# Attention: three kinds of store on another queue, a gating row loaded and used in one unit, more filler steps at the start, the last squares on another engine

## The chip, the cores and the metric

The kernel runs on one core of one Trainium2 chip. The core has five engines with instruction queues of their own: TensorE (PE: matmuls and transposes, with its weight loads shown as PEld), VectorE (DVE), ScalarE (ACT), GpSimd (POOL) and SyncE (SP, which only issues DMAs here). The metric is the device time of one execution in microseconds (us).

## The reference, cut to what matters

One layer: a norm, a combined input projection, three causal attention branches a, b and c, a gate and an up-projection for each, a merge by sigmoid gates gm, an output projection with a residual add and a last norm. SEQ and D_MODEL are 1024.

```python
h = rms_norm(x, norm_gain[l], RMS_EPS)
proj = jnp.einsum('bsd,de->bse', h, w_in[l])          # q, k, v, gates of a, b, c, and gm
ya = diff_attention(...)                              # 4 heads, two softmaxes each, width 128
ya = (rms_norm(ya, subln_gain[l], SUBLN_EPS) * (1.0 - lam_init)).reshape(B, S, A_WIDTH)
yb = sliding_window_attention(...)                    # 8 heads, window 128
yc = forgetting_attention(...)                        # 8 heads, decay by cumulated log gates
ua = jnp.einsum('bse,ed->bsd', ya * jax.nn.silu(ga), w_up_a[l])
ub = jnp.einsum('bse,ed->bsd', yb * jax.nn.silu(gb), w_up_b[l])
uc = jnp.einsum('bse,ed->bsd', yc * jax.nn.silu(gc), w_up_c[l])
gates = jax.nn.sigmoid(gm.reshape(B, S, N_BRANCH, D))
merged = gates[:, :, 0] * ua + gates[:, :, 1] * ub + gates[:, :, 2] * uc
x = x + jnp.einsum('bsd,de->bse', merged, w_o[l])
```

## The kernel before

Matmul operands are split into a high and a low part, so that most products are three matmuls (high by high, low by high, high by low). The program has three stretches: norm and projections, to about 518 us of the profile; attention, to 962 us, with 28 filler steps ahead of it from 518 us on; and up-projections, merge, output projection and last norm. The change lies in the attention stage.

**Units.** Attention runs over a list of units: 16 of part b (two groups of heads by eight row blocks), 32 of part c (eight heads by four pairs of row blocks) and 16 of part a (four heads h by pairs g = 3, 2, 1, 0). A unit is a list of score steps (L630 or L755 on PE, the maximum and mask on DVE in L650 or L757, the exponential on ACT), a list of transposes (L676, with the cast pt on ACT and the rest pt on DVE, L683) and a list of products with v (L709). The loop over units runs the scores of unit n beside the transposes and products of unit n - LAG, LAG being 2, so that the first two units have scores alone and the last two passes have none. Inputs q, k and v of a head are loaded some units ahead by SP (L608, L620) into buffers that are given free by PE.

**Fillers.** 16 tiles of the gm gates are left over from the projection stage and computed in between: `fillers()` is a generator of 256 steps of three matmuls each (L531 to L533). FILL_0 = 28 steps stand ahead of the first unit; then each step of a unit earns a fraction of a filler step (FILL_B, FILL_C, FILL_A by part), until FILL_END = 8 are left, which are kept for the last two passes. A finished half row is copied by ACT to gr (L537) and stored to gmd by DMA (L538).

**Gates of branch b.** When the last half rows have been computed (`cur["free"]`), the eight gating rows of branch b are worked off, GPART = 2 entries of the list gq at the head of each unit. `gate_load` (L560) loads a row of y (yd_b) into a buffer of tag y_st, and a row of silu values (sgd) into a buffer of tag w_st, in which filler weights are loaded too. `gate` multiplies them on DVE (L567), ACT casts the product (L101) and DVE takes the rest (L104). The list puts the load of row n + 1 ahead of the gate of row n.

**End of a unit of part a.** `store` in `part_a`: ACT copies the result to ya (L857), a DMA stores it to yd_a (L859), POOL squares it (L861), ACT casts the squares, POOL takes the rest (L104), and NSUM cost units later PE sums them by two matmuls (L867); ACT copies the sums (L868), and a DMA stores them to ssd (L869). gr, ya, y2, y_lo and the gating row share the five buffers of tag y_st.

**Order.** PE's instructions run in the order in which the program issues them. On the other engines the order is a scheduler's, so that an edit of one line can move others. All DMAs named here are issued by SP. Eight semaphores are shared by the DMAs in turn, and an issue waits until the DMA that had its semaphore before has landed.

Of the kernel before, what the change touches and what calls it, by code (L numbers as in the profile page):

```python
# [12 lines left out]
ALU = mybir.AluOpType  # L13
# [3 lines left out]
P = 128  # L17
# [18 lines left out]
LAG, AHEAD, TVLAG = 2, 3, 1  # L36
# [2 lines left out]
NLAST, GPART, NY, NSUM = 6, 2, 5, 8.0  # L39
GATE_AT = {"b": (0, 1, 2, 3, 4, 4, 5, 5), "c": (1, 1, 2, 2, 3, 4, 5, 5)}  # L40
FILL_END, FILL_Z = 8, 1.5
FILL_0, FILL_B, FILL_C, FILL_A = 28, 0.8, 0.6, 0.75
NPW, UPAHEAD, WARM = 3, 3, 14
UPS = [(br, d) for br in "bca" for d in range(NK)]
WO_AT = {5 + 2 * n: (m, t) for n, (m, t) in enumerate((m, t) for m in ((0, 0), 3, 2, (1, 0)) for t in range(2))}
# [4 lines left out]
def hybrid_block_kernel(ctx, tc, x, norm_gain, w_in, b_forget, lambda_q1, lambda_k1, lambda_q2, lambda_k2,  # L50
                        subln_gain, sinks, w_up_a, w_up_b, w_up_c, w_o, final_gain, out):
    nc = tc.nc
# [45 lines left out]
    def split(src, hi, lo, act=False, eng=nc.gpsimd):  # L98

        if act:  # L100
            first = nc.scalar.copy(hi, src)  # L101
        else:
            first = nc.gpsimd.tensor_scalar(out=hi, in0=src, scalar1=1.0, scalar2=1.0, op0=ALU.mult, op1=ALU.mult)
        return first, eng.tensor_tensor(lo, src, hi.bitcast(F32), ALU.subtract)  # L104
# [414 lines left out]
    def fillers():  # L519


        for tiles, halves in ([([t], (1, 0)) for t in DIRECT[:-NLAST]] + [(DIRECT[-NLAST:], (1,)), (DIRECT[-NLAST:], (0,))]):
            for bi, d in tiles:
                w = [operand(load_half(GM + bi * D + d * P, i)) for i in range(2)]
                for c in halves:
                    ps = cur["psum"]()
                    for i in range(2):
                        for k in range(4):
                            f, l = i == 0 and k == 0, i == 1 and k == 3
                            r = hb[i, c]  # L530
                            nc.tensor.matmul(ps, w[i][0][:, k, :], r[0][:, k, :], start=f, stop=False)  # L531
                            nc.tensor.matmul(ps, w[i][0][:, k, :], r[1][:, k, :], start=False, stop=False)
                            nc.tensor.matmul(ps, w[i][1][:, k, :], r[0][:, k, :], start=False, stop=l)  # L533
                            if l:
                                pool, tg, nb = cur["row"]
                                gr = pool.tile([P, 512], F32, name="gr", tag=tg, bufs=nb)
                                nc.scalar.copy(gr, ps)  # L537
                                nc.sync.dma_start(gmd[bi, d, :, c * 512:c * 512 + 512], gr)  # L538
                            yield
            if halves == (1,):  # L540
                cur["free"] = True
# [36 lines left out]
    with tc.tile_pool(name="at", bufs=2, reuse_waits="tile") as at, \  # L578
# [14 lines left out]
        def fill(n):  # L593
            owed[0] += n
            while owed[0] >= 1:
                owed[0] -= 1
                if left[0] > cur["keep"]:
                    left[0] -= 1
                    next(filler)
# [228 lines left out]
        def part_a(u, h, g):  # L828
# [25 lines left out]
            def store(y):  # L854

                ya = at.tile([P, 512], F32, name="ya", tag="y_st", bufs=NY)
                nc.scalar.copy(ya[:, :256], y[:, :256])  # L857
                cols = slice(g * 256, g * 256 + 256)
                nc.sync.dma_start(yd["a"][h * P:h * P + P, cols], ya[:, :256])  # L859
                y2 = at.tile([P, 2, 256], F32R, name="y2", tag="y_st", bufs=NY)  # L860
                nc.gpsimd.tensor_tensor(ya[:, 256:], ya[:, :256], ya[:, :256], ALU.mult)  # L861
                split(ya[:, 256:], y2[:, 0, :], y2[:, 1, :], True)

                def sums():
                    pn = cur["psum"]()
                    for t in range(2):
                        nc.tensor.matmul(pn[:2, :256], ones, y2[:, t, :], start=t == 0, stop=t == 1)  # L867
                    nc.scalar.copy(ya[:1, :256], pn[:1, :256])  # L868
                    nc.sync.dma_start(ssd[h:h + 1, cols], ya[:1, :256])  # L869
                after(NSUM, sums)  # L870
            ta, va = pv_pair(g, w, lhs, 3, store)
            return sa, ta, va, lambda: None
# [56 lines left out]
        def tick(c):  # L929
            clock[0] += c  # L930
            for e in list(later):
                if e[0] <= clock[0]:
                    later.remove(e)
                    e[1]()
        gq = [gb[0][0]] + [f for n in range(8) for f in ([gb[n + 1][0]] if n < 7 else []) + [gb[n][1]]]
        for n in range(len(units) + LAG):
            if "free" in cur:
                if "b" not in yg:
                    gate_tiles("b")
                for f in gq[:GPART]:  # L940
                    f()
                del gq[:GPART]

            while ahead < min(n + AHEAD + 1, len(units)):
                if units[ahead][0]:
# [23 lines left out]
            while sa or tv:  # L969
                if sa and (not tv or (ps_ + 0.5 * sa[0][0]) * ct <= (pt_ + 0.5 * tv[0][0]) * cs):  # L970
                    c, f = sa.pop(0)
                    ps_ += c
                else:
                    c, f = tv.pop(0)
                    pt_ += c
                f()
                if n < len(units):
                    fill(c * rate[kind] / 0.65)
                else:
                    cur["keep"] = 0  # L980
                    fill(c * FILL_Z / 0.65)
                tick(c * (1 + rate[kind]))
        for _, f in later:
            f()

# [170 lines left out]
```

## Time and profile before

| what | before |
|---|---|
| median of 3 timed runs | 1188.73 us (1188.29 to 1191.81) |
| profiled execution, its own time | 1184.62 us |
| its span, first to last instruction | 1182.8 us |
| mean granted clock of TensorE | 0.991 |
| PE busy | 1147.9 us, 97% |
| DVE busy | 815.4 us, 69% |
| POOL busy | 693.8 us, 59% |
| ACT busy | 585.5 us, 50% |

All times in the rows are microseconds from the start of the span, durations included, unless marked ns. Busy time of an engine is time in instructions that compute. A bracket at the end of a row, as [1.18 <-DMA qk<-qd], is the time for which the engine stood idle before it, and what ended the wait. Names read out<-in by the program's tiles. A granted clock of 1.00 is 2.4 GHz, one of about 0.5 is 1.2 GHz. SPq and ACTq are the queues from which SP and ACT issue DMAs.

### The profile page before, as it was taken

To read this page: it belongs to the slowest core of one execution; us is meant where nothing else is said; L and a number is where in the kernel's file an instruction comes from. 1 tells how busy PE (TensorE), PEld (TensorE's weight loads), DVE (VectorE), ACT (ScalarE), POOL (GpSimd) and SP (SyncE) were. 2 spreads that over 40 slices of the span, in tenths; PEclk is the share of its full clock that TensorE was granted. 3 is DMA by queue.
4 is the path that set the end of the run, shared out by engine and by line. 5 is a ranking of instruction groups with operands and counts; after the bars stand their busy time and mean duration, and the time that the engine had idled before them with its cause. 6 is when DMAs were issued, how large, how long until landed. Compare 5 with 4: busy or idle time off the path is not lost. (4 is left out here: it accounts for less than half of the span.)

```text
span 1182.8 us, 18767 instructions
## 1 busy us (share of the span) xinstructions
PE 1147.9 (97%) x5787; PEld 972.6 (82%) x5787; DVE 815.4 (69%) x1655; ACT 585.5 (50%) x1255; POOL 693.8 (59%) x684
## 2 busy tenths in 40 slices
PE   7999999999999999998999999999998999999997
PEld 6999888888888888887888888888877878888775
DVE  7767767768687775322887767768677835664898
ACT  6432333433444444323886666667877842334423
POOL 5056656657667676454556665766767732477643
PEclk8999999999999999999999999999999999999999
DMA  7442266666856555349946466466668359798322
GB/s 242 155 153 91 103 209 230 233 213 198 266 185 205 166 164 161 99 117 247 258 117 194 133 191 183 134 176 172 176 205 234 121 163 337 271 345 306 129 107 107
DMA packets 184531, 221.70 MB, mean 187 GB/s; under 512 B 16280, under 2 KB 116712, under 8 KB 182640
## 3 DMA queue, kind: packets, MB, share of 16 engines
q1 hardware_dynamic: 184288, 219.99, 58.9%
q8 instruction: 46, 0.75, 0.3%
q14 instruction: 53, 0.43, 0.1%
q10 hardware_dynamic: 144, 0.52, 0.1%
HBM read 144.89 MB, written 75.56 MB: 186 GB/s over the span
## 5 line engine op out<-in xcount | busy, mean ns | idle before, releaser
L104 POOL TENSOR_TENSOR w_lo<-w_st,w_hi 128x512 fp32r<-128x512 f32 x130 | 173.4, 1340 | 108.5 <-ACT w_hi L101 89.4
L104 POOL TENSOR_TENSOR w_lo<-w_sf,w_hi 128x512 fp32r<-128x512 f32 x96 | 143.2, 1494 | 104.8 <-ACT w_hi L101 84.4
L109 PE MATMUL pm<-t,w_hi 128*128 128x512 f32 x320 | 126.3, 395 | 0.7 <-ACT w_hi L101 0.7
L111 PE MATMUL pm<-t,w_lo 128*128 128x512 f32 x320 | 126.3, 395 | 0.0
L110 PE MATMUL pm<-t,w_hi 128*128 128x512 f32 x320 | 126.0, 394 | 0.0
L630 PE MATMUL sc<-qk 128*128 128x512 f32 (+2 forms) x384 | 101.9, 356 | 3.7 <-DVE m L650 3.7
L683 DVE TENSOR_TENSOR pt<-tp,pt 128x512 fp32r<-128x512 f32 x102 | 70.1, 687 | 23.8 <-ACT pt L682 23.0
L169 DVE TENSOR_TENSOR w_sf<-w_st 128x512 f32<-128x512 f32 x40 | 47.7, 1193 | 43.5 <-DMA w_st<-in_w_in_dram 34.8
L630 PEld LDWEIGHTS sc<-qk 128*128 128x128 f32 x384 | 64.6, 189 | 15.3 <-DVE m L650 6.8
L101 ACT CAST w_hi<-w_sf 128x512 fp32r<-128x512 f32 x96 | 58.5, 613 | 35.4 <-PE pm L110 29.5
L109 PEld LDWEIGHTS pm<-t,w_hi 128*128 128x128 f32 x320 | 60.1, 188 | 14.9 <-ACT w_hi L101 1.1
L110 PEld LDWEIGHTS pm<-t,w_hi 128*128 128x128 f32 x320 | 60.1, 188 | 14.1
L111 PEld LDWEIGHTS pm<-t,w_lo 128*128 128x128 f32 x320 | 60.1, 188 | 14.1
L101 ACT CAST w_hi<-w_st 128x512 fp32r<-128x512 f32 x86 | 51.3, 615 | 37.6 <-PE pm L110 28.5
L682 ACT CAST pt<-tp 128x512 fp32r<-128x512 f32 x102 | 59.4, 582 | 20.4 <-PE tp L676 18.8
L423 ACT ACTIVATE qk_hi<-u 128x512 fp32r<-128x512 f32 x32 | 20.2, 633 | 94.2 <-DVE u L191 43.9
L664 POOL TENSOR_SCALAR e_c<-e_c,r 128x1024 f32<-128x1024 f32 (+3 forms) x64 | 47.9, 749 | 23.8 <-DVE r L658 20.0
L709 PE MATMUL y<-pt,v 128*128 128x256 f32 x336 | 55.4, 290 | 2.4 <-DVE pt L683 2.2
L656 ACT ACTIVATE e_c<-e_c,m 128x1024 f32<-128x1024 f32 (+3 forms) x64 | 49.9, 780 | 13.7 <-DVE m L650 12.8
L840 POOL TENSOR_TENSOR e_a<-e_a,e_a 128x896 f32<-128x896 f32 (+7 forms) x32 | 47.3, 1481 | 15.9 <-ACT e_a L839 15.8
L656 ACT ACTIVATE e_a<-e_a,m 128x896 f32<-128x896 f32 (+7 forms) x64 | 49.6, 775 | 13.3 <-DVE m L650 13.1
L1048 POOL TENSOR_TENSOR mt<-mt,row 128x512 f32<-128x512 f32 x28 | 39.5, 1426 | 24.7 <-DVE row L1047 24.6
(299 smaller groups left out, 3511.4 us busy)
## 6 DMA issues: line engine op xcount, KB each, us to landing
w_st<-in_w_in_dram SPq DMA_DIRECT2D x126, 256.0 KB, 3.4
qk<-qd SPq DMA_DIRECT2D x224, 128.0 KB, 3.1
wo<-wod SPq DMA_DIRECT2D x14, 1024.0 KB, 9.0
row<-gmd SPq DMA_DIRECT2D x48, 256.0 KB, 4.5
qd<-qk_hi SPq DMA_DIRECT2D x42, 256.0 KB, 4.1
qd<-qk_lo SPq DMA_DIRECT2D x42, 256.0 KB, 4.9
vd<-vt SPq DMA_DIRECT2D x24, 384.0 KB, 2.3
v<-vd SPq DMA_DIRECT2D x9, 1024.0 KB, 9.8
```

Source lines behind the costliest of these rows:

```text
L101: first = nc.scalar.copy(hi, src)
L104: return first, eng.tensor_tensor(lo, src, hi.bitcast(F32), ALU.subtract)
L109: nc.tensor.matmul(ps, w[0][:, k, :], r[0][:, k, :], start=start and k == 0, stop=False)
L110: nc.tensor.matmul(ps, w[0][:, k, :], r[1][:, k, :], start=False, stop=False)
L111: nc.tensor.matmul(ps, w[1][:, k, :], r[0][:, k, :], start=False, stop=stop and k == n - 1)
L169: nc.vector.tensor_tensor(t, x, y, op)
L630: nc.tensor.matmul(ps[:, :n], q, kk[t][c][:, o:o + n], start=t == 0, stop=t == 1)
L656: nc.scalar.activation(e[:, :L], e[:, :L], AF.Exp, bias=m2, scale=-1.0, accum_out=den)
L664: nc.gpsimd.tensor_scalar(out=e, in0=e, scalar1=r, scalar2=1.0, op0=ALU.mult, op1=ALU.mult)
L682: nc.scalar.copy(pt[:, 0, a:], tp[:, a:])
L683: nc.vector.tensor_tensor(pt[:, 1, a:], tp[:, a:], pt[:, 0, a:].bitcast(F32), ALU.subtract)
L709: nc.tensor.matmul(y[:, :256], l_, r_, start=t == 0 and n == 0, stop=last and n == len(mms) - 1)
```

## The change

Three kinds of DMA are issued by ACT instead of SP: gr to gmd (32 of them), ya to yd_a (16) and the sums to ssd (16). In the list of gates the load of a row stands at the head of a unit and its gate at the end of the same unit, one row per unit. In the first two units a fixed number of two filler steps stands behind each of the eight score steps, and FILL_B and FILL_A are a little lower. In the last two units of part a (h = 3, g < 2) the squares and their rest are done by DVE instead of POOL.

```diff
-FILL_0, FILL_B, FILL_C, FILL_A = 28, 0.8, 0.6, 0.75
+FILL_0, FILL_S, FILL_B, FILL_C, FILL_A = 28, 2, 0.75, 0.6, 0.74
...
                                 nc.scalar.copy(gr, ps)
-                                nc.sync.dma_start(gmd[bi, d, :, c * 512:c * 512 + 512], gr)
+                                nc.scalar.dma_start(gmd[bi, d, :, c * 512:c * 512 + 512], gr)
...
-                nc.sync.dma_start(yd["a"][h * P:h * P + P, cols], ya[:, :256])
+                nc.scalar.dma_start(yd["a"][h * P:h * P + P, cols], ya[:, :256])
                 y2 = at.tile([P, 2, 256], F32R, name="y2", tag="y_st", bufs=NY)
-                nc.gpsimd.tensor_tensor(ya[:, 256:], ya[:, :256], ya[:, :256], ALU.mult)
-                split(ya[:, 256:], y2[:, 0, :], y2[:, 1, :], True)
+                eng = nc.vector if h == 3 and g < 2 else nc.gpsimd
+                eng.tensor_tensor(ya[:, 256:], ya[:, :256], ya[:, :256], ALU.mult)
+                split(ya[:, 256:], y2[:, 0, :], y2[:, 1, :], True, eng)
...
                     nc.scalar.copy(ya[:1, :256], pn[:1, :256])
-                    nc.sync.dma_start(ssd[h:h + 1, cols], ya[:1, :256])
+                    nc.scalar.dma_start(ssd[h:h + 1, cols], ya[:1, :256])
...
-        gq = [gb[0][0]] + [f for n in range(8) for f in ([gb[n + 1][0]] if n < 7 else []) + [gb[n][1]]]
+        gq = [f for n in range(8) for f in gb[n]]
         for n in range(len(units) + LAG):
+            gnow = []
             if "free" in cur:
                 if "b" not in yg:
                     gate_tiles("b")
-                for f in gq[:GPART]:
+                gnow = gq[:2]
+                del gq[:2]
+                for f in gnow[:1]:
                     f()
-                del gq[:GPART]
...
                 f()
-                if n < len(units):
+                if n < LAG:
+                    fill(FILL_S)
+                elif n < len(units):
                     fill(c * rate[kind] / 0.65)
...
+            for f in gnow[1:]:
+                f()
```

PE at the start of attention, the first scores of part b (L755) and the filler steps (L531 to L533, h10 being an input tile of theirs); the piece of the difference, with what is new marked:

```order
 L755 MATMUL sc<-kb_5029,qk 128x256
 L755 MATMUL sc<-kb_5032,qk 128x256
+L531 MATMUL pj<-h10h,w_hi 128x512
+L532 MATMUL pj<-h10l,w_hi 128x512
+L533 MATMUL pj<-h10h,w_lo 128x512
+L531 MATMUL pj<-h10h,w_hi 128x512
+L532 MATMUL pj<-h10l,w_hi 128x512
+L533 MATMUL pj<-h10h,w_lo 128x512
+L755 MATMUL sc<-kb_5029,qk 128x256
+L755 MATMUL sc<-kb_5032,qk 128x256
```

The same pattern of six filler matmuls and a score goes on through the first two units; before, four scores (eight matmuls) stood in a row with one filler step behind them.

DVE in part a, around the fourth gate (L567), before:

```order
1282 L683 TENSOR_TENSOR pt<-tp,pt 128x512
1283 L650 ISA e_a_10556,m<-sc,posA 128x512
1284 L650 ISA m 128x1
1285 L658 RECIPROCAL r<-den 128x1
1286 L838 COPY dens<-den 128x1
1287 L683 TENSOR_TENSOR ptz_5011<-tp,ptz_5011 128x384
1288 L650 ISA e_a_10597,m<-sc,posA 128x512
1289 L650 ISA m 128x1
1290 L567 TENSOR_TENSOR gate<-gate 128x512
```

and the same place in the changed kernel, with the fifth and the sixth gate (the fourth stands some 40 rows higher there):

```order
1284 L683 TENSOR_TENSOR pt<-tp,pt 128x512
1285 L567 TENSOR_TENSOR gate<-gate 128x512
1286 L104 TENSOR_TENSOR yg_b_9938<-gate,yg_b_9937 128x512
1287 L650 ISA e_a_10625,m<-sc,posA 128x512
1288 L650 ISA m 128x1
1289 L567 TENSOR_TENSOR gate<-gate 128x512
1290 L658 RECIPROCAL r<-den 128x1
1291 L838 COPY dens<-den 128x1
1292 L104 TENSOR_TENSOR yg_b_9938<-gate,yg_b_9937 128x512
1293 L683 TENSOR_TENSOR ptz_5011<-tp,ptz_5011 128x384
```

The gate stands directly behind the pt subtraction and ahead of two scores, where it stood behind them.

SP around the loads for the last head of part a (L608, L620) and the gating rows (L560), before:

```order
499 L608 DMA qk<-qd 64x512 x6
500 L620 DMA v<-vd 128x8x256
501 L608 DMA qk<-qd 64x512 x6
502 L560 DMA gate<-yd_b 128x512
503 L859 DMA yd_a<-ya 128x256
504 L869 DMA ssd<-ya 1x256
505 L560 DMA gate<-sgd 128x512
506 L141 DMA w_st<-in_w_in_dram 128x4x128
507 L560 DMA gate<-yd_b 128x512
```

and in the changed kernel:

```order
453 L608 DMA qk<-qd 64x512 x5
454 L620 DMA v<-vd 128x8x256
455 L608 DMA qk<-qd 64x512 x7
456 L560 DMA gate<-yd_b 128x512
457 L141 DMA w_st<-in_w_in_dram 128x4x128 x2
458 L560 DMA gate<-yd_b 128x512
```

The stores are gone from between, and the gating rows stand behind the same burst of q, k and v.

ACT in part a of the changed kernel, with what each instruction waits for (DMAHW0 and the like are the semaphores that the DMAs share):

```order
790 L857 COPY ya<-y 128x256 [waits DMAHW5_49]
791 L682 CAST ptz_5011<-tp 128x384 [waits PE_49]
792 L859 DMA yd_a<-ya 128x256 [waits DMAHW0_49,Activation_49]
793 L656 ACTIVATE e_a_10057,den<-e_a_10057,m 128x512 [waits DVE_49]
794 L101 CAST y_9974<-ya 128x256 [waits Pool_49]
795 L537 COPY gr<-pj 128x512 [waits PE_49]
796 L101 CAST yg_b_9935<-gate 128x512 [waits DVE_49]
797 L538 DMA gmd<-gr 128x512 [waits DMAHW4_49,Activation_49]
```

The stores (L859, L538) are new in this queue; before, only the copies, casts and exponentials stood in it.

Where the filler steps run out: counted in PE's order at the same matmul of part a, 238 steps are done before and 248 (all but the eight kept ones) in the changed kernel; before, the 248th stands 65 rows later. At the beginning of part c the changed kernel is 11 steps ahead.

## Rows read from the trace of the kernel before

**Rows 1.** Page, busy us, share of the span, instructions of each engine

```profile
PE 1147.9 (97%) x5787; PEld 972.6 (82%) x5787; DVE 815.4 (69%) x1655; ACT 585.5 (50%) x1255; POOL 693.8 (59%) x684
```

**Rows 2.** Timeline of PE, attention's start: start, us, engine, line, [idle before <-releaser]

```profile
550.42 0.47 PE L755 MATMUL sc<-kb,qk 128*128 128x256 f32 x2 [1.18 <-DMA qk<-qd]
553.17 0.77 PE L755 MATMUL sc<-kb,qk 128*128 128x256 f32 x2 [2.27 <-DMA qk<-qd]
553.74 0.63 PE L531 MATMUL pj<-h10h,w_hi 128*128 128x512 f32 x1
...
557.00 0.39 PE L531 MATMUL pj<-h10h,w_hi 128*128 128x512 f32 x1
```

**Rows 3.** Windows: length, busy of PE, PEld, DVE, ACT, POOL, clock, DMA share, GB/s

```profile
518.00:549.00 31.00, 31.00 (x139) 25.52 (x137) 4.05 (x6) 6.20 (x9) 16.65 (x21) 1.00 0.72 191
540.00:560.00 20.00, 16.39 (x76) 13.31 (x74) 4.95 (x27) 7.99 (x25) 5.74 (x10) 0.91 0.89 241
549.00:962.00 413.00, 398.48 (x2401) 344.05 (x2400) 298.45 (x966) 296.74 (x719) 263.34 (x368) 1.00 0.61 176
924.50:949.00 24.50, 24.20 (x153) 20.67 (x154) 19.96 (x73) 22.23 (x54) 18.50 (x16) 1.00 0.36 114
962.30:966.30 4.00, 4.00 (x12) 3.15 (x11) 0.00 (x0) 0.00 (x0) 0.00 (x0) 0.57 0.65 158
```

**Rows 4.** Timeline of PE, two filler matmuls late in part a

```profile
956.21 0.40 PE L531 MATMUL pj<-h10h,w_hi 128*128 128x512 f32 x1
956.44 0.39 PE L532 MATMUL pj<-h10l,w_hi 128*128 128x512 f32 x1
```

**Rows 5.** Timeline of ACT at the program's start, its one DMA issue

```profile
0.74 0.41 ACTq L385 DMA_DIRECT2D gain<-in_norm_gain_dram  x1
```

**Rows 6.** Timeline of DVE and PE, two holes in part a

```profile
886.15 1.37 DVE L567 TENSOR_TENSOR gate<-gate 128x512 f32<-128x512 f32 x1
...
888.19 0.73 PE L630 MATMUL sc<-qk 128*128 128x512 f32 x2 [2.62 <-DVE m L650]
...
907.68 0.90 DVE L567 TENSOR_TENSOR gate<-gate 128x512 f32<-128x512 f32 x1 [1.46 <-DMA gate<-yd_b]
...
909.24 0.86 PE L709 MATMUL y<-pt,v 128*128 128x256 f32 x5 [2.15 <-DVE pt L683]
```

**Rows 7.** Timeline of SP and DVE around the last head's loads

```profile
894.82 3.79 SPq L608 DMA_DIRECT2D qk<-qd  x6
...
898.20 0.68 DVE L683 TENSOR_TENSOR pt<-tp,pt 128x512 fp32r<-128x512 f32 x1
...
898.66 0.57 SPq L560 DMA_DIRECT2D gate<-yd_b  x1
...
903.93 0.69 DVE L567 TENSOR_TENSOR gate<-gate 128x512 f32<-128x512 f32 x1 [1.28 <-DMA gate<-yd_b]
```

**Rows 8.** Timeline of SP and DVE near the second gate's new place

```profile
863.46 0.23 SPq L869 DMA_DIRECT2D ssd<-ya  x1
...
864.98 0.69 DVE L683 TENSOR_TENSOR pt<-tp,pt 128x512 fp32r<-128x512 f32 x1
```

**Rows 9.** Timeline of ACT and SP at 854 us; page, DMA issues (KB, us to landing)

```profile
854.45 0.35 ACT L857 COPY ya<-y 128x256 f32<-128x256 f32 x1
854.53 3.14 SPq L608 DMA_DIRECT2D qk<-qd  x5
...
qk<-qd SPq DMA_DIRECT2D x224, 128.0 KB, 3.1
```

**Rows 10.** Attention's end: PE's waits (us, times, longest), timeline of POOL, DVE; DVE's groups

```profile
PE pj L867 <- POOL y L104: 1.5, 2, 1.0
PE pj L867 <- ACT y L101: 0.8, 1, 0.8
...
960.68 0.72 POOL L104 TENSOR_TENSOR y<-ya,y 128x256 fp32r<-128x256 f32 x1 [0.59 <-ACT y L101]
...
968.86 0.69 DVE L567 TENSOR_TENSOR gate<-gate 128x512 f32<-128x512 f32 x1 [13.49 <-DMA gate<-yd_c]
...
L650 DVE CUSTOM_DVE_ANT_0 e_a<-sc,posA 128x256 f32<-128x256 f32 x8 | 3.3, 416 | 0.3 <-PE sc L630 0.3
```

## Prediction

> **What bounds the kernel now.** I read the busy times of the engines first. TensorE (PE) works 1147.9 us of a span of 1182.8 us, 97% [rows 1]: this kernel is a queue of matmuls, and the end comes earlier only if PE waits less or runs less of its work at the lower clock. The change leaves PE's 5787 matmuls the same and moves none but the filler ones among them. So the sum needs only PE's idle time and its slow stretches, and every other engine counts only where it makes PE wait. The second view was the list of what PE waited for, the third its timeline around the larger waits. Inside the attention stage there are four such places that the change touches: its start at 549 us, two holes at 886 and 907 us, and its end at 958 us. The fourth view, busy time by stretch, says what else could become the bound: over the attention stage PE is busy 398.5 of 413 us, ScalarE (ACT) 296.7 and VectorE (DVE) 298.5 [rows 3], so on average there is room on both, but between 924.5 and 949 us ACT is busy 22.2 of 24.5 us [rows 3], and there is almost none.
>
> **Start of attention: 16 filler steps instead of 2 in the first two units.** Right behind the 28 fillers that stand ahead of the stage, PE runs score matmuls whose key rows are still on their way: it waits 1.18 us and then 2.27 us for the DMA that brings qk [rows 2]. After the second wait a filler matmul takes 0.63 us instead of 0.39 us [rows 2], and the granted clock of 540 to 560 us is 0.91 [rows 3]: the clock fell to 1.2 GHz. Slow time lasts from 553.17 to 557.00 us, 3.83 us, in which PE did what takes half as long at 2.4 GHz; that costs some 1.85 us. With two filler steps (six matmuls at about 0.23 us, 1.4 us) behind each score of these units, the four scores of the first unit are spread over some 7 us, until about 556, and every qk row that they need landed by 553.2 [rows 2]. The fillers' own operands are no wait that I can see: PE ran through the 31 us ahead, most of them fillers, without a hole [rows 3]. So I book 1.18 + 2.27 + 1.85 = **-5.3 us**; if the clock falls anyway it is -3.5.
>
> **Those fillers are missing later.** The supply is fixed. By the two PE orders the changed kernel is 10 to 11 steps ahead from part c on, and its last free filler (8 are kept for the end in both) stands where 238 steps are done now: about 924.5 us. Behind that point the kernel before has 10 more steps until about 942 us, 30 matmuls at 0.235 us (start to start, [rows 4]), 7.05 us of PE's 24.2 [rows 3]. If nothing else needed the time, the stretch would become 7 us shorter and all would be even. But ACT works 22.23 us of those 24.5 [rows 3]: without 0.7 us for copies of filler results, and with about seven DMA issues that now stand in its queue, it needs 21.5 us if an issue costs it nothing and 24.4 us at 0.41 us each, the one DMA that ACT issues in the kernel before [rows 5]. So the stretch shrinks by 0.1 to 3 us and PE idles 4 to 7 us. I take **+5**.
>
> **Gates at the end of a unit.** Two of PE's holes come from the present order. At 886.15 us DVE's gate takes 1.37 us behind another slow operation, a softmax step is late, and PE waits 2.62 us; at 907.68 us DVE has sat 1.46 us for a gating row, the subtraction behind it is late, and PE waits 2.15 us [rows 6]. The gates move by some score steps (they stand behind steps 48, 51, 58, 68, 69, 74, 78, 89 of part a's 96 now, and 44, 45, 48, 55, 66, 67, 72, 82 then), so both holes go: -4.8 us. But the new places have their own rows to wait for. The fifth gate comes to stand directly behind DVE's pt subtraction of 898.20 us, which ends at 898.88. Its row is issued by SP behind the whole burst of q, k and v of the last head, and that burst begins only when PE releases buffers; in the trace the row behind the burst (the fourth gate's there) is issued at 898.66 and used at 903.93, after DVE had sat 1.28 us for it [rows 7]. If the row comes at the same time, DVE stands 903.93 - 898.88 = 5.05 us instead of 1.28, with the subtraction, two scores and two reciprocals queued behind it. The 1.28 us hold cost PE nothing, the 1.46 us one cost it 2.15 [rows 6]; from a hold of 5 us I take PE's wait as 3.5 us (0 to 5.05). The sixth gate now stands one score behind it, with its row issued behind two weight loads, and the second gate stands just behind the pt subtraction of 864.98, while its row needs a y_st buffer that is given free by a store issued at 863.46 and then has to land itself [rows 8]. Each could hold DVE about as long as the row of 907.68 did. I take +3 for both (0 to 5.4). Net: -4.8 + 3.5 + 3 = **+1.7**, bounds -4.8 to +5.7.
>
> **Stores from ACT's queue.** 64 issues leave SP and stand between ACT's copies, casts and exponentials: at 0.41 us [rows 5] some 26 us more on an engine with 116 us of room in the stage [rows 3], so on average hidden by PE, whose matmuls go on; the bare stretch is the one booked above. What is not hidden is that such an issue also waits for the earlier DMA on its semaphore, and the order shows that most of these are loads that SP issues. In nearly all cases that load was issued more than 3 us before. In one it was not: ya is copied at 854.45, and the store's semaphore belongs to a qk load out of a group that begins at 854.53 [rows 9]. A qk load lands some 3.1 us after issue (page's median, [rows 9]), so ACT would stand up to 2.8 us there, and pt casts behind it. I take **+1** (0 to 2.8).
>
> Here the Trainium skill speaks against a gain: "DMA: Bandwidth & Descriptors", section "Issuing engines are not separate DMA queues", says that DMAs started by different engines run on the same 16 engines and that issuing from several saves only the time of the issue. By this rule the gating rows would come when they came, and the gates' term stays at +1.7; if a queue without stores did bring them in time, the term would be -4.8 and the sum -5.3. The trace before has no store from ACT, so no row here decides it.
>
> **Last squares on DVE.** At the end of part a PE waits 1.5 us for POOL's y and 0.8 us for ACT's y [rows 10], since POOL does the squares and the low parts of the last two units (0.72 us for one) behind a weight split, while DVE has nothing to do until 968.86 [rows 10]. DVE's operation of 128x256 out of SBUF isn't in the trace; its score of that size takes 0.42 us [rows 10]. Four operations shorter by some 0.3 us, and no split ahead of them: **-1.2**. The bounds are 0, if the casts on ACT end last, and -2.8, if the hole closes so far that the clock, 0.57 in the four us behind it [rows 3], stays up.
>
> **Sum.** -5.3 + 5 + 1.7 + 1 - 1.2 = +1.2 us. The profiled execution took 1184.62 us, so it would take 1185.8; the median of the timed runs is 1188.73, 4.1 us above the profiled one, and I carry the difference over: 1188.73 + 1.2, about **1190**.
>
> **Rivals.**
> *A, faster: the gating rows come in time.* The holes of rows 6 vanish and no new ones come, because SP, free of 64 stores, issues the rows early enough: -5.3 + 4 - 4.8 + 0 - 1.2 = -7.3, 1181.4 us. For it: 64 stores, each of which waits for ACT's copy, are gone from ahead of the rows. Against it: the row behind the last head's burst is not delayed by a store at all, the burst stands ahead of it in both orders, and it took 5.3 us from issue to use [rows 7].
> *B, slower: the fifth gate holds DVE so long that PE's clock falls.* Place: 899 to 909 us. Price: gates at their upper bound +5.7, the fall once more 1.85 as at the start, fillers at their full 7.05: -5.3 + 7.05 + 5.7 + 1.85 + 1 - 1.2 = +9.1, 1197.8 us. It decides as soon as PE idles there about as long as the 2.27 us that ended in the slow clock at 553 [rows 2]; against it, the hole of 2.62 us at 888 was followed by a score at full rate [rows 6].
> *C, slower: ACT becomes the bound.* Its issues cost 0.41 us and hold it at two or three places by 2 to 3 us, so the bare stretch loses all of 7.05 and the rest +5: -5.3 + 7.05 + 1.7 + 5 - 1.2 = +7.3, 1196 us. For it: ACT's 22.2 of 24.5 us [rows 3]. Against it: over the whole stage it is idle 28%.
> *D: the change doesn't do what it says,* as the stores still share the transfer engines and the semaphores with SP's loads, and the rows land when they did. That is the forecast's own assumption for the gates, and gives no time of its own.
>
> **How the numbers follow.** A difference under 0.3% (3.6 us) can't be told from none with this kernel. The forecast, +1.2, holds with 0.38 for a time within 3.6 us of the time before; A and what lies between it and the forecast 0.32; B 0.14; C 0.16. So faster 0.32, same 0.38, slower 0.30. The range goes from A's 1181.4, a little inside, to B's 1197.8: 1182 to 1197. The forecast's own range is 1185 to 1192.5.
>
> **What would show it.** Start: no wait of PE for qk near 549 us, and a granted clock of 1.00 there. Fillers: PE busy clearly less than 24.2 of 24.5 us in the last 20 us ahead of the last two units, waits named after ACT's or DVE's tiles, the stretch hardly shorter. Gates: DVE's gate waits for the DMA of yd_b with 4 to 5 us at the fifth, and a PE hole of 3 us behind it; if that wait is under 1 us, A is right. ACT: waits at its DMA issues released by loads. End: PE's waits at the sums fall from 2.3 us to about 1. I would be wrong above all if ACT's work ahead of the bare stretch moved forward with the stretch, so that the missing fillers cost 2 instead of 5, or if a store held ACT where I see none.

## The result, and the profile after

The changed kernel takes 1195.18 us (median of 8 runs, 1191.49 to 1197.13), the kernel before 1188.34 us in the same runs (median of 8): a ratio of 1.0057, with a 95% interval of 1.0037 to 1.0077. So the change makes the kernel 6.8 us slower. The time lies in the stated range (1182 to 1197) and above the forecast's own range (1185 to 1192.5): of the four cases a slower one came, to which the text gave 0.30.

The profiled execution took 1196.6 us with a span of 1194.8 us, 12.0 us more than the span of before. That is more than the medians differ, since the profiled execution of before (1184.62 us) was among the fastest of its kernel and that of after among the slower ones of its own; terms read from these two traces are good to a few us in sum. Page of the changed kernel, busy us by engine, to be held against [rows 1]:

```profile
PE 1152.3 (96%) x5787; PEld 975.2 (82%) x5787; DVE 805.7 (67%) x1659; ACT 588.2 (49%) x1255; POOL 691.2 (58%) x680
```

The work is the same, the waits are others. What PE waited for in the changed kernel (us in total, times, longest):

```profile
PE pj L868 <- ACT gr L537: 8.4, 1, 8.4
PE sc L630 <- DVE m L650: 3.9, 8, 1.4
PE pj L868 <- ACT y L101: 3.5, 2, 2.2
...
PE y L780 <- ACT pt L682: 2.1, 1, 2.1
```

The waits for qk at the start and the two holes of [rows 6] are gone, and one wait of 8.4 us, for ACT's copy of a filler result, stands out.

To see where the 12 us arise I matched the matmuls that are no fillers one by one in the two traces, took the difference of their start times, and took off 0.70 us for each filler step by which the changed kernel is ahead at that point (three matmuls at 0.235 us, [rows 4]). Times in the first column are those of the kernel before.

| stretch | difference | what it is |
|---|---|---|
| 549 to 568 us | -5.3 | start: no wait for qk, clock up |
| 568 to 575 | +4.4 | ACT stands at a store |
| 575 to 862 | +2.0 | several small ones |
| 862 to 868 | +3.9 | ACT stands at a store |
| 868 to 897 | +0.2 | second and third gate; the hole at 886 |
| 897 to 899 | +9.7 | the 8.4 us hole and the slow clock behind it |
| 899 to 928 | -1.6 | the hole at 907 is gone |
| 928 to 952 | +4.4 | fillers missing |
| 952 to 966 | -2.8 | sums at the end |
| 966 to the end | -2.8 | up-projection and later, whose program is not edited |

The stage itself, to 966 us, stands at +14.9, more than twice the 6.8 us of the medians. A second trace of the same kernel, from the repeat at the end of the experiments, gives -5.5, +3.7, +3.3, +2.2, +0.2, +9.6, -1.7, +4.5, -2.8 and -2.8 for the same ten stretches: the hole, the start and the end come again within 0.3 us, the two holds of ACT within 1.7. The last stretch comes again too: waits of PE for weights of the output projection, which the kernel before has near 1100 and 1140 us, are gone in both. The part on the squares comes back to it.

The windows of the changed kernel (columns as in [rows 3]) show the start and the stretch without fillers:

```profile
540.00:560.00 20.00, 20.00 (x96) 16.67 (x95) 3.41 (x17) 7.33 (x19) 7.19 (x10) 1.00 0.92 270
...
903.00:921.00 18.00, 8.94 (x49) 7.55 (x50) 8.62 (x26) 9.56 (x20) 8.99 (x10) 0.83 0.75 216
944.00:968.50 24.50, 21.58 (x141) 17.94 (x140) 18.49 (x73) 22.76 (x57) 16.26 (x16) 1.00 0.17 56
```

From 540 to 560 us PE is busy all of 20 us at full clock, against 16.39 at 0.91 [rows 3]. In the 18 us around the hole it works half the time and the clock falls to 0.83. From 944 us on PE is busy 21.58 of 24.5 us and ACT 22.76, against 24.20 and 22.23 [rows 3].

**The hole of 8.4 us.** The timelines of DVE, ACT, PE and SP of the changed kernel at that place (start, us, engine, line):

```profile
912.11 0.33 SPq L560 DMA_DIRECT2D gate<-yd_b  x1
...
916.05 0.69 DVE L567 TENSOR_TENSOR gate<-gate 128x512 f32<-128x512 f32 x1 [4.13 <-DMA gate<-yd_b]
...
916.78 0.62 ACT L101 CAST yg_b<-gate 128x512 fp32r<-128x512 f32 x1 [2.67 <-DVE gate L567]
918.15 0.59 ACT L537 COPY gr<-pj 128x512 f32<-128x512 f32 x1 [0.76 <-DVE yg_b L104]
...
918.79 0.58 PE L868 MATMUL pj<-y,ones 128*2 128x256 f32 x2 [8.37 <-ACT gr L537]
919.17 1.05 PE L630 MATMUL sc<-qk 128*128 128x512 f32 x2
```

The row is issued at 912.11, behind the last head's burst, and DVE's gate waits 4.13 us for it. The next step is what the forecast didn't follow: ACT's cast of the gate waits for DVE, and behind that cast in ACT's queue stands the copy of a filler result, which gives a buffer of PSUM (the memory that PE writes into) free. PE's next matmul needs that buffer. So PE stands from 910.42, 1.5 us before DVE's wait begins, and until 918.79, 2.7 us behind its end, since the gate (0.69), the cast (0.62), DVE's rest (0.69) and the copy (0.59) follow one behind the other: 8.37 us for a DVE wait of 4.13. The last row of ACT shows a second link: the copy itself waited 0.76 us for DVE's rest of the gate (L104). That rest is the last to read the gating row, whose buffer is of the five of tag y_st that gr shares. So the copy may have needed that buffer too, and a place further ahead in ACT's queue might not have been enough; this was not tried.

**The two holds of ACT.** Timeline of SP (first row) and ACT in part b and part a of the changed kernel:

```profile
569.32 3.88 SPq L608 DMA_DIRECT2D qk<-qd  x5
...
574.96 0.34 ACTq L538 DMA_DIRECT2D gmd<-gr  x1
575.35 0.51 ACT L760 ACTIVATE eb<-eb,m 128x256 f32<-128x256 f32 x1 [4.49 <-DMA qk<-qd]
...
872.22 0.33 ACTq L859 DMA_DIRECT2D yd_a<-ya  x1
872.60 0.72 ACT L656 ACTIVATE e_a<-e_a,m 128x512 f32<-128x512 f32 x1 [2.17 <-DMA qk<-qd]
```

Each time ACT stood idle ahead of a store, and what ended it was a load that SP had issued: the store waits for the load that had its semaphore before. By the semaphores in the trace, the load behind the first hold is the one that SP issued at 569.32, 5.6 us before the store could go. The pt casts and exponentials behind it were late, and PE waited in part b for pt (2.1 us) and in part a for y (2.2 us). That such loads can land so late could have been read from the trace before, where the loads of q and k (L608) show:

```profile
DMA to landing us min/median/max: 2.4/3.1/8.3
```

### The profile page after: what moved, and what is told of

It reads as the page before. It is cut to its first block, busy times and chain, and to the rows that moved or that the text cites. A ratio compares the mean times of both kernels' runs of the same rounds, so it can differ in the third digit from the quotient of the medians.

```text
span 1194.8 us, 18718 instructions
## 1 busy us (share of the span) xinstructions
PE 1152.3 (96%) x5787; PEld 975.2 (82%) x5787; DVE 805.7 (67%) x1659; ACT 588.2 (49%) x1255; POOL 691.2 (58%) x680
## 4 chain that ended last, share of the span: by engine, by line
PE 84%; DVE 6%; DMA 3%; ACT 2%; issue 2%; POOL 2%; SPq 0%; DVEq 0%; ACTq 0%; POOLq 0%
PE pm L109 11%; PE pm L111 11%; PE pm L110 11%; PE p L111 6%; PE p L109 6%; PE p L110 6%; PE y L709 4%; PE tp L676 4%; PE pj L532 4%; PE sc L630 4%; PE pj L531 4%; PE pj L533 4%; PE pm L312 3%; PE pm L313 3%; PE pm L314 3%
## 5 line engine op out<-in xcount | busy, mean ns | idle before, releaser
L104 POOL TENSOR_TENSOR w_lo<-w_st,w_hi 128x512 fp32r<-128x512 f32 x130 | 173.6, 1341 | 111.9 <-ACT w_hi L101 99.7
L104 POOL TENSOR_TENSOR w_lo<-w_sf,w_hi 128x512 fp32r<-128x512 f32 x96 | 144.5, 1508 | 97.4 <-ACT w_hi L101 93.2
L109 PEld LDWEIGHTS pm<-t,w_hi 128*128 128x128 f32 x320 | 60.1, 188 | 14.9 <-ACT w_hi L101 1.1
L664 POOL TENSOR_SCALAR e_c<-e_c,r 128x1024 f32<-128x1024 f32 (+3 forms) x64 | 48.2, 753 | 21.2 <-DVE r L658 15.9
L709 PEld LDWEIGHTS y<-pt,v 128*128 128x128 f32 x336 | 48.2, 190 | 8.4 <-DVE pt L683 3.5
```

Of the source, the lines that this page charges most:

```text
L109: nc.tensor.matmul(ps, w[0][:, k, :], r[0][:, k, :], start=start and k == 0, stop=False)
L664: nc.gpsimd.tensor_scalar(out=e, in0=e, scalar1=r, scalar2=1.0, op0=ALU.mult, op1=ALU.mult)
L709: nc.tensor.matmul(y[:, :256], l_, r_, start=t == 0 and n == 0, stop=last and n == len(mms) - 1)
```

## Experiments

Theories at the beginning. **G**: the new list of gates puts a gate in front of a row that isn't there. **F**: the fillers' lead does, since the gates begin when the fillers' last half rows are done. **S**: stores on ACT's queue hold ACT until loads of SP have landed. All ratios are to the kernel before in the same runs. The experiments ran in three groups, each on a chip of its own with the kernel before beside them. So two changed kernels of different groups are held against each other by their ratios, not by their medians.

**Only the fillers** (and their rates):

```diff
-FILL_0, FILL_B, FILL_C, FILL_A = 28, 0.8, 0.6, 0.75
+FILL_0, FILL_S, FILL_B, FILL_C, FILL_A = 28, 2, 0.75, 0.6, 0.74
...
-                if n < len(units):
+                if n < LAG:
+                    fill(FILL_S)
+                elif n < len(units):
```

> Only the fillers change: two filler steps behind each of the first eight scores, and the two lower rates; stores on SP, gates in the old list, squares on POOL. The sum's own terms give -5.3 at the start and +5 where the fillers are missing, so about 0 if the gates' new places come from the new list of gates (theory G). But the fillers also finish earlier, and with them the gates start a unit earlier: in this kernel's order a gate stands directly behind the pt subtraction with its row behind the last head's burst of q, k and v, just as in the whole change. If that is what opened the 8.4 us wait of TensorE there (theory F), this kernel shows the wait too, of 5 us or more near 905 us, and is 4 to 8 us slower than the kernel before.

Measured: 1202.06 us, ratio 1.0128 (1.0104 to 1.0153), 15 us slower, more than the 4 to 8 expected of F and more than the whole change. DVE and PE in its trace, with stores on SP and the old list:

```profile
912.75 0.69 DVE L567 TENSOR_TENSOR gate<-gate 128x512 f32<-128x512 f32 x1 [4.87 <-DMA gate<-yd_b]
...
915.50 0.59 PE L867 MATMUL pj<-y,ones 128*2 128x256 f32 x2 [9.01 <-ACT gr L537]
```

The hole is there, so F holds: being 11 steps ahead, the gates begin two units earlier in the program, and the scheduler sets one directly behind the pt subtraction, its row behind the burst. By the same matching this kernel gains 5.2 us at the start, and loses 7.3 us between 853 and 872, 10.3 by 904 and 7.3 where fillers are missing (928 to 945).

**Only the list of gates:**

```diff
-        gq = [gb[0][0]] + [f for n in range(8) for f in ([gb[n + 1][0]] if n < 7 else []) + [gb[n][1]]]
+        gq = [f for n in range(8) for f in gb[n]]
```

(with the load at a unit's head and the gate at its end, as in the change)

> Only the list of gates changes: load at a unit's head, gate at its end. Theory G (the list brings the gates' new waits): DVE's gate waits for yd_b by 4 us or more near the last head's loads and TensorE stands 5 to 8 us, so +2 to +6 us. Theory F (the early fillers bring them): the gates stand within a few instructions of their old places, the wait stays near 1.3 us and the time within 2 us of the kernel before.

Measured: 1187.77 us, ratio 1.0007 (0.9987 to 1.0027), no difference. The gates of DVE near the burst in its trace:

```profile
900.27 0.69 DVE L567 TENSOR_TENSOR gate<-gate 128x512 f32<-128x512 f32 x1 [0.68 <-DMA gate<-yd_b]
904.94 1.01 DVE L567 TENSOR_TENSOR gate<-gate 128x512 f32<-128x512 f32 x1 [2.39 <-DMA gate<-yd_b]
```

They stand where they stood, and wait 0.68 and 2.39 us where it was 1.28 and 1.46 [rows 6, 7]. G falls for the list by itself; the list beside the fillers' lead was not run without the squares (see below).

**Only the stores** on ACT's queue, all three kinds:

```diff
-                                nc.sync.dma_start(gmd[bi, d, :, c * 512:c * 512 + 512], gr)
+                                nc.scalar.dma_start(gmd[bi, d, :, c * 512:c * 512 + 512], gr)
```

(and the same for yd_a and ssd)

> Only the queue of the three kinds of store changes. Theory S (an issue on ScalarE is held until an earlier load of SP's has landed, and casts behind it come late): ScalarE stands 2 to 4.5 us at one to three stores with a load named as what ended it, TensorE waits some 2 to 8 us more, the time is +2 to +8 us. Rival (the issues are hidden, and the holds seen in the whole change come from the earlier fillers): no hold above 1 us and within 2 us of the kernel before.

Measured: 1193.68 us, ratio 1.0063 (1.0040 to 1.0086), 7.5 us slower. What ended ACT's waits in its trace from 520 to 980 us, transfers alone:

```profile
ACT ya L868 <- DMA qk<-qd: 4.0, 1, 4.0
ACT e_c L656 <- DMA v<-vd: 2.5, 1, 2.5
```

S holds: without any change of gates or fillers ACT stands 4.0 and 2.5 us behind stores until a load lands. In the kernel before, no wait of ACT for qk or v is over 1.0 us in that stretch.

**Only the stores of filler results** (32 of the 64):

> Of the whole change only the 32 stores of filler results are on ScalarE's queue; the stores of ya and of the sums stay on SP. The three kinds of store together cost 7.5 us; in that trace TensorE had lost some 2 us in part b, 2 us in part c, where only filler results are stored, and the rest in part a. If each hold is a store's own, this costs 3 to 5 us. Rival: the stores of ya and the sums do the harm, then it is within 2 us of the kernel before.

Measured: 1195.05 us, ratio 1.0070 (1.0040 to 1.0100), 8 us slower, as much as all three kinds: my 3 to 5 was too low, and the harm does not go by the number of stores. Timeline of SP (first row) and ACT in part c, and the window behind it (columns as in [rows 3]):

```profile
724.17 0.54 SPq L620 DMA_DIRECT2D v<-vd  x1
...
731.45 0.33 ACTq L538 DMA_DIRECT2D gmd<-gr  x1
731.82 0.61 ACT L656 ACTIVATE e_c<-e_c,m 128x384 f32<-128x384 f32 x1 [2.87 <-DMA v<-vd]
```

```profile
732.00:748.00 16.00, 14.85 (x80) 12.98 (x80) 10.42 (x32) 9.06 (x21) 7.66 (x14) 0.89 0.47 124
```

One hold of 2.87 us, which ends with the v load issued 7.3 us before, cost 3.7 us in the matching, with a granted clock of 0.89 behind it. In part a this kernel lost some 7 us more; there ACT's copy of sums waited 3.8 us for a ya store of SP, and PE 2.1 us for that copy. Whether that comes from the moved stores or from the scheduler's other order was not told apart.

**Only the squares** on DVE:

```diff
-                nc.gpsimd.tensor_tensor(ya[:, 256:], ya[:, :256], ya[:, :256], ALU.mult)
-                split(ya[:, 256:], y2[:, 0, :], y2[:, 1, :], True)
+                eng = nc.vector if h == 3 and g < 2 else nc.gpsimd
+                eng.tensor_tensor(ya[:, 256:], ya[:, :256], ya[:, :256], ALU.mult)
+                split(ya[:, 256:], y2[:, 0, :], y2[:, 1, :], True, eng)
```

> Only the last two units' squares and their low parts go from POOL to DVE. The forecast's term was -1.2 us; the trace of the whole change shows TensorE 2.8 us nearer from 952 to 966 us, so -1 to -3 us if the gain is the squares' own, and 0 if it only came from an engine that had waited longer before.

Measured: 1181.52 us, ratio 0.9959 (0.9943 to 0.9974), 4.9 us faster, more than the 1 to 3 expected: the one part of the change that gains by itself. PE at the sums in its trace:

```profile
959.27 0.82 PE L868 MATMUL pj<-y,ones 128*2 128x256 f32 x4
961.28 0.28 PE L868 MATMUL pj<-y,ones 128*2 128x256 f32 x1 [1.20 <-ACT y L101]
961.75 0.28 PE L868 MATMUL pj<-y,ones 128*2 128x256 f32 x1 [0.18 <-DVE y L104]
```

Two waits of 1.4 us in all are left of 2.3 [rows 10], and no matmul behind them runs slowly. At the place itself the matching gives -2.9 us. Behind 966 us it gives -2.8 more, as in the whole change, since these waits of the kernel before are gone (us in total, times, longest):

```profile
PE p L109 <- ACT w_hi L101: 1.4, 2, 0.9
...
PE p L111 <- POOL w_lo L104: 0.2, 1, 0.2
```

So the 4.9 us (interval 3.1 to 6.8) lie in two places, less 1.6 us by which this trace stands behind at 952 us. That the second place is the squares' doing is not shown: its waits are gone in six of the eight traces with the squares on DVE, but also in one of the six with the squares on POOL (early fillers paid back), which has a granted clock of 1.00 behind the sums as well and gains 2.5 us there.

**The whole change, with the gating rows' loads at a higher priority** in the scheduler, which moves the fifth row ahead of most of the burst:

```diff
                 for f in gnow[:1]:
-                    f()
+                    with tc.high_priority():
+                        f()
```

> The whole change, with the loads of the gating rows given a higher priority in the scheduler, so that the fifth row stands among the first loads of the last head's burst and not behind it; nothing else is edited. Theory H: the hole of 8 to 9 us in TensorE's row comes from that row landing late (DVE's gate holds, ScalarE's cast of the gate waits behind it, the copy that empties the fillers' PSUM buffer stands behind that cast). Then DVE's wait there falls under 2 us, TensorE's wait for gr vanishes, and the time is 5 to 9 us less than that of the whole change, 1186 to 1190 us. Rival: the hole is ScalarE's stores held by SP's loads; then it stays, or moves, and the time stays within 2 us of the whole change's.

Measured: 1191.27 us, ratio 1.0044 (1.0026 to 1.0062). The hole of 8.4 us is gone from its trace; PE's largest waits from 880 to 925 us are these:

```profile
894.65 0.50 PE L630 MATMUL sc<-qk 128*128 128x256 f32 x2 [1.99 <-DVE m L650]
...
910.58 0.40 PE L868 MATMUL pj<-y,ones 128*2 128x256 f32 x2 [2.55 <-ACT gr L537]
```

So the row behind the burst makes the hole. By the ratios the gain is 1.5 to 5 us (from 1.0057 or, in the repeat, 1.0086), at the best the low end of the 5 to 9 that I expected: part of the hole comes back as the 2.55 and the 1.99.

**The whole change without the moved stores** (all on SP again):

> The whole change but for the stores, which are issued by SP as before. Theory S (each store on ScalarE waits for an earlier load of SP's; the stores alone cost 7.5 us): 4 to 8 us faster than the whole change, 1186 to 1191 us. Rival (with the early fillers SP's queue is what makes the gating rows late, and the stores on ScalarE take that away): slower than the whole change, 1195 to 1202 us, near the fill edit alone less the squares' gain.

Measured: 1191.70 us, ratio 1.0035 (1.0016 to 1.0055), by the ratios 2.6 to 6 us less than the whole change, where I expected 4 to 8 of S. The hole stays, at 8.89 us:

```profile
915.04 0.59 PE L868 MATMUL pj<-y,ones 128*2 128x256 f32 x2 [8.89 <-ACT gr L537]
```

and the loss of 4.4 us in part b is gone: the matching stands at -5.0 us at 596 us, where the whole change stands at -1.0. This kernel also says something of the list: it is the fillers' kernel (1.0128) with the new list and the squares added, and 11 us faster, of which the squares alone give 4.9. Beside the fillers' lead the list may then be a gain; which it is was not told apart.

**Both at once: rows at a higher priority, stores on SP**; and the **whole change again**, beside it:

> The whole change with its stores back on SP's queue and the gating rows' loads at the higher priority. The kernel without the moved stores still had the 8.9 us hole and was 4 us slower than before; the row ahead in the burst took the hole away in the whole change. Theory H (row behind the burst) and theory S (stores on ScalarE hold it) are two causes in different places, so both gains should add: no hole of TensorE above 3 us near the last head's loads, no hold of ScalarE at a store, 1181 to 1186 us. Rival: with the stores among the loads on SP the rows are late all the same; then the hole stays and the time is 1190 us or more.

> The whole change once more, unchanged, so that it stands on the same chip beside these kernels: 0.4 to 0.8% slower than the kernel before, and the hole of about 8 us in TensorE's row near 910 us again. If its time is within 2 us of the kernel with the rows at higher priority, the hole is worth less than its length.

Measured: 1186.57 us, ratio 1.0004 (0.9984 to 1.0025), and 1195.35 us, ratio 1.0086 (1.0055 to 1.0116), with the hole again in the latter:

```profile
PE pj L868 <- ACT gr L537: 8.2, 1, 8.2
```

The first was expected at 1181 to 1186 and came out a little above. The four kernels form a square of ratios to the kernel before:

| | stores on ACT | stores on SP |
|---|---|---|
| row behind the burst | 1.0057 and 1.0086 | 1.0035 |
| row ahead | 1.0044 | 1.0004 |

The row ahead gives 1.5 to 5 us with the stores on ACT and 3.7 with them on SP; the stores back on SP give 2.6 to 6 us with the row behind and 4.7 with it ahead. Each ratio is good to some 0.2 to 0.3%, so single cures are clear of noise only in part. Both together give 8.8 us by the medians of the one chip on which both ran. So the loss has these two causes, and the traces show them in different places; that their sizes simply add fits, but isn't shown to the us. What is left beside them can be read from the last kernel's matching: -5.1 at the start, -2.9 at the sums and -2.8 behind 966 us are used up by +5.3 for the missing fillers (928 to 952), +6.3 between 853 and 928, where the earlier gates stand, and +1.8 before that.

**The early fillers, paid back inside part b**, alone and with the squares:

```diff
-FILL_0, FILL_B, FILL_C, FILL_A = 28, 0.8, 0.6, 0.75
+FILL_0, FILL_S, FILL_B, FILL_C, FILL_A = 28, 2, 0.53, 0.6, 0.75
```

> Only the 16 early filler steps, and FILL_B lowered to 0.53 so that the 11 steps are paid back inside part b; from part c on the fillers stand where they stood in the kernel before, and the gates begin at their old unit. The terms: -5.3 at the start, nothing at part a's end, and 0 to +3 in part b, where ScalarE and VectorE are busy 86 to 90%. If the fillers' lead is what made the fill edit alone 15 us slower, this kernel is 2 to 5 us faster than the kernel before. Rival: fewer fillers in part b cost there what the start gains; then it is within 2 us.

> The kernel of the early fillers paid back inside part b, with the last two units' squares on DVE as well. The squares alone gave -4.4 us; if the two gains lie in different places and don't touch each other, this is 4 to 5 us faster than the early fillers alone, 6 to 10 us faster than the kernel before, 1176 to 1180 us. Rival: the end of the stage is bound by something else as soon as the start is earlier, then only one of the two gains is left.

Measured: 1194.45 us, ratio 1.0074 (1.0049 to 1.0098), and 1198.51 us, ratio 1.0090 (1.0061 to 1.0119). Both misses: I expected a gain. Two things went wrong. In part b the gain of the start went: the matching falls from -6.5 us at 575 to -1.2 at 637, though PE has 13 matmuls fewer to do there. The window of this kernel and that of the kernel before, from 596 to 637 us:

```profile
596.00:637.00 41.00, 40.12 (x224) 32.71 (x223) 34.74 (x115) 33.05 (x91) 24.84 (x46) 1.00 0.44 115
```

```profile
596.00:637.00 41.00, 41.00 (x237) 35.46 (x237) 34.68 (x115) 33.11 (x94) 24.93 (x45) 1.00 0.42 116
```

DVE and ACT do the same work in the same time. What PE's weight loads wait for in this stretch, and don't wait for in the kernel before, are the exponentials that POOL scales (L664) ahead of the transposes:

```profile
PEld tp L676 <- POOL eb L664: 2.8, 10, 0.3
```

That is 2.8 of the 3.5 us that the matching loses here; before, fillers stood in these gaps. So a filler that is taken out of such a stretch gives little time back. And in part a the order of the gates changed all the same, though they begin at the old unit; a hole came at the same burst, of another make:

```profile
907.08 0.36 ACT L868 COPY ya<-pj 1x256 f32<-1x256 f32 x1 [2.82 <-DMA yd_a<-ya]
907.49 0.80 PE L531 MATMUL pj<-h00h,w_hi 128*128 128x512 f32 x1 [4.00 <-ACT ya L868]
```

The store of ya that ACT's copy of sums waits for stands behind the burst on SP. So the position of the gates' start alone does not set this; the scheduler's whole order there does. The kernel with the squares added is 0.16% slower than the one without, less than either's interval, but the 4 to 5 us that I expected are not there. The end of part a could not give them: the kernel without the moved squares already gains 2.5 us there. The rest of the difference stays open.

**The squares, and the rows at a higher priority, on the kernel before:**

```diff
-            ts[n] = gate_load(br, n % 4, n // 4)
+            with tc.high_priority() if br == "b" else ExitStack():
+                ts[n] = gate_load(br, n % 4, n // 4)
```

> The kernel before with the last two units' squares on DVE and with the gating rows' loads at the higher priority, and nothing else of the change: no early fillers, the old list of gates, stores on SP. The squares alone gave -4.4 us. The second late row of the kernel before cost TensorE 2.2 us near 909 us; if rows come ahead of the burst that wait goes too: -5 to -7 us, 1180 to 1182 us. Rival: the loads ahead in the queue make the scores' own rows late, which gives it back: -2 to -5 us.

Measured: 1186.54 us, ratio 0.9996 (0.9973 to 1.0019): the squares' gain is lost again, and the time lies outside both ranges that I gave. Timeline of SP and PE, where PE waits 2.82 us for q or k itself:

```profile
915.31 2.39 SPq L609 DMA_DIRECT2D qk<-qd  x4
...
921.80 0.76 PE L631 MATMUL sc<-qk 128*128 128x512 f32 x1 [2.82 <-DMA qk<-qd]
```

The load is one of the head's last four, which SP issues from 915.31 on and issued from 910.95 on in the kernel before. That fits the rival, that rows ahead make the scores' own rows late; but the order of SP changed in other ways too, and the two were not told apart. The fastest of all kernels run is the one before with the squares on DVE, 1181.52 us.

## Why the prediction was right, and where it was not

The range held and the sum's sign was right, but the sum was +1.2 where +6.8 came, so the likeliest case was not the one that came. That the time fell inside the range is in part luck: the traces put the gates and the stores at 8.3 us each, beyond the bounds of both (5.7 and 2.8), and the 2.8 us behind 966 that took some of it back were in no term. Step by step:

- **Start, -5.3.** Measured -5.3; granted clock 1.00, no wait for qk. The kernels without early fillers stand between -2.3 and +1.4 at the same place, so the agreement to the tenth is chance.
- **Missing fillers, +5.** Measured +4.4 in the whole change. ACT is the busiest engine there (22.76 of 24.5 us), as the text argued; but PE's own waits in that window name tiles of POOL (1.2 us) and DVE (1.7 us), so that ACT sets the pace is argued and not shown.
- **Gates, +1.7 (bounds -4.8 to +5.7).** This step failed. The row, the place and DVE's wait were right (4.13 us, against 5.05 from the rows), but 8.3 us came in sum, from 868 to 928 us. Two things were missed. The 3.5 us for PE were judged by what had stood behind DVE; ACT's queue, with the gate's cast ahead of the copy that empties PE's buffer, made 8.37 of it, plus 1.3 us in the slow clock: the rival B's mechanism and price, but through ACT. And the cause was put down to the new list of gates: that list alone changes nothing (1.0007), and the fillers' lead alone brings the hole.
- **Stores, +1 (0 to 2.8).** Mechanism right, size off. The hold of 854 us came (2.17 us, expected up to 2.8), but cost PE 3.9, and another of 4.49 us came in part b: 4.4 us. What the term had wrong is the landing: it took the page's median of 3.1 us and counted every semaphore as free whose load had been issued more than 3 us before, but in that same trace loads of q and k took up to 8.3 us, and the one behind the hold of part b took 5.6. Alone the stores cost 7.5 us. Holds at two or three places were rival C's mechanism; whether the issues themselves, 0.2 to 0.5 us each, cost anything was not told apart from them.
- **Squares, -1.2 (0 to -2.8).** Measured -2.8: the upper bound, since the clock stayed up (1.00 in the four us behind the sums, 0.57 before [rows 3]). DVE's operation took 0.42 to 0.43 us, as estimated, once 0.69. By itself this edit gave 4.9 us, with a second place behind 966 us that the sum did not have.

The Trainium skill's rule from "DMA: Bandwidth & Descriptors", "Issuing engines are not separate DMA queues", that another issuing engine saves only the issue time, agrees with the runs: with the stores gone from SP's queue the gating row still was late (issued at 912.11, used at 916.05). That the kernels with the stores on SP are 2.6 to 7.5 us faster lies in what the issues wait for, of which that sentence says nothing.

## What to carry to other kernels

When work is moved ahead in a queue that others are timed by, look at what starts when it ends: here the fillers' earlier end moved the gates, and that cost more than the wait that was filled. Follow a held instruction through every engine that queues behind it until a buffer of the bound engine turns up, not only through its own engine's queue. Before moving a store to a compute engine's queue, look at what its issue waits for: if it shares semaphores with loads of another queue, the compute engine waits for these loads, and for the latest of them, not for the median one.

## What the runs showed of the hardware

The clock falls behind holes of very different lengths: after the 8.37 us hole the matmuls at 920 us took 0.63 us instead of 0.39, and the clock was 0.89 in the 16 us behind a hold that made PE wait only 1.4 us at once in the kernel with the filler stores moved. At 888 us in the kernel before, a hole of 2.62 us was followed by a score at full rate [rows 6], with a granted clock of 1.00 from 888 to 892. In these traces the length of one hole does not tell it. A move of 64 stores, 0.2 to 0.5 us each to issue, cost 7.5 us, and a move of 32 of them 8 us: the cost does not go by their number. And loads of one kind and size (128 KB of q or k) landed 2.4 to 8.3 us after their issue in the kernel before, with a median of 3.1.
